# The last mLSTM head's transposed output goes from PSUM to the output projection's operands, without a round trip through DRAM

## The chip, the cores and the metric

The kernel runs on one core of one Trainium2 chip. The metric is the device time of one execution in microseconds (us). Three runs of the kernel before gave 1370.7, 1372.6 and 1374.29 us, so its median is 1372.6 us.

## What is computed

One layer of a bidirectional encoder: a combined input projection, then an attention group of 8 heads beside an mLSTM group of 4 heads, one output projection over both, and a gated feed-forward network. Cut to what matters here (1024 tokens, width 1024, mLSTM heads of 128):

```
y_attn = axial_gqa_attention(q_a, k_a, v_a, ...)                 # 512 features
h = h_fw + h_bw                                                  # per mLSTM head, 1024 x 128
h = h * rsqrt(mean(h * h) + EPS) * norm_g * sigmoid(o_pre)       # y_mem: 4 heads, 512 features
mix = concatenate([y_attn, y_mem]) @ w_out                       # the output projection
x = x + g1 * mix
h = modulate(rms_norm(x, norm_ffn_g), sh2, sc2)                  # then the feed-forward network
```

Products are made to nearly fp32 accuracy from three passes: each operand is split into a high part (rounded to fp32r) and a low part (what is left), and high x high, low x high and high x low are added up in PSUM.

## The kernel before

A Python planner writes the order of every engine's instructions: streams of matmul work (`ck.streams`) are merged by a clock with assumed costs, and chains of small steps (`ck.chain`) are put on the queues of ScalarE (ACT), VectorE (DVE), GpSimd (POOL) and SyncE (SP) as the planner's clock reaches them. The hardware then runs each engine's list strictly in that order. A step whose data are late holds up everything behind it on its engine.

**The output projection.** `MIX` (L49) lists its 32 units. A unit makes 128 output features for 512 tokens: 4 groups (k = 0 to 3) of 3 matmuls, one group for each 128 input features. The first 16 units take the attention half of the input, the last 16 the mLSTM half. In this text, unit 1.f is the mLSTM unit of feature block f (0 to 7) for tokens 512 to 1023, and unit 0.f the same for tokens 0 to 511. The planned order is: the attention units, then 1.0 to 1.7, then 0.0 to 0.7. `load_y` (L1229) provides the operands of one token half: for each k it loads a 128 x 512 tile `yat` from DRAM (`ya_d` for attention, `ym_d` for the mLSTM heads, k being the head), ACT makes the high part `yah`, POOL the low part `yal`. The weights come as `wst` from DRAM, with `whi` made by ACT and `wlo` by DVE, several units ahead. When a unit is done, DVE adds its bank into the residual (`x<-acc,mod,x`), SP stores the sum to DRAM for later (`x_d<-x`), and ACT and DVE gather the sum of squares (`sq`, `ssq`) from which the matmul `ms<-ssq` makes the mean for the second norm.

**The end of an mLSTM head.** `last` (L2010) is the chain for one head and one token half b: DVE forms `hs` from numerators and denominators, ACT squares it, DVE reduces to `ss`, POOL takes the root, and DVE multiplies by root and gate (`hs<-hs,ss,so`, four pieces). `transposed` (L2057) then turns the four 128 x 128 blocks on TensorE (PE) into one PSUM bank `tr`, ACT copies the bank, scaled by `mlstm_norm_g`, to the tile `ymt`, and SP stores that to `ym_d`. The flag `ym_ok[h][b]` releases the load in `load_y`. In `ends` (L2085) b = 1 comes before b = 0. The fourth head (h = 3) is the last one, and its turning of b = 1 lies directly ahead of the units that need it as k = 3.

**PSUM.** While the mLSTM part runs, the 8 banks are one pool with 2 banks for `acc`, 2 for `acct`, 1 for `tr` and 3 others (L2195). When the mLSTM streams are at their end (L2216) and the unit then under way is done, that pool is closed and a new one with 8 banks for `acc` is opened (L2226). The first unit planned behind that point waits for the readers of the old pool.

## Time and profile before

| what | value |
|---|---|
| three runs, median | 1372.6 us |
| the profiled execution, its own time | 1369.04 us |
| its span in the trace | 1367.2 us |
| mean granted TensorE clock | 0.983 of full |
| DVE busy | 1050.5 us (77%) |
| ACT busy | 709.6 us (52%) |
| POOL busy | 648.0 us (47%) |

The profile is one execution. Instructions carry the line of kernel.py that issued them; ACT, DVE and POOL instructions all go through one helper (L98), so they are told apart by the names of their tiles, output before input. Rows of the timeline give the start, the duration, the engine, line, operation, tiles and shapes, and in brackets how long the engine had stood idle and what released it. Consecutive matmuls overlap: in steady work at the full clock a 128x512 matmul is listed with 0.39 us, but the next one starts 0.23 us later. The time outside of the span, 1369.04 - 1367.2 = 1.84 us, is start and end.

### The profile page before, as it was taken

What the parts mean: (1) busy time and instruction counts of PE and PEld (TensorE: products, weight loads), DVE (VectorE), ACT (ScalarE), POOL (GpSimd) and SP (SyncE); (2) the same over time, 40 slices, a digit from 0 to 9 for tenths busy, and PEclk for the clock granted to TensorE, in tenths of its full rate; (3) what the DMA queues carried; (4) which work ended last, traced back from release to release, by engine and by line L of the source; (5) the groups of instructions that cost most, each with busy time, mean ns of one, the idle gap of its engine ahead of it and who ended that gap; (6) DMA issues with size and microseconds to landing.
All of it is one profiled execution on the core that took longest, in us unless ns stands there. A gap on an engine that the chain in (4) does not pass through costs nothing.

```text
span 1367.2 us, 19584 instructions
## 1 busy us (share of the span) xinstructions
PE 1278.0 (93%) x6596; PEld 1071.4 (78%) x6596; DVE 1050.5 (77%) x1599; ACT 709.6 (52%) x1344; POOL 648.0 (47%) x538
## 2 busy tenths in 40 slices
PE   7898888899999989999999999999999999979997
PEld 5786666788778879787778788888888887857887
DVE  7936698975789748989588989867666754998866
ACT  6575366778577755555377522333323334344462
POOL 0352577655667524443215255545555445545442
PEclk9999999999999999999899999999999999989999
DMA  9544333233233236763553344332333159623324
GB/s 360 160 132 129 112 106 92 88 99 107 66 94 111 65 120 199 255 202 115 179 181 116 101 143 150 123 108 100 108 108 116 71 187 349 249 78 107 100 59 158
DMA packets 105043, 188.07 MB, mean 138 GB/s; under 512 B 11632, under 2 KB 33264, under 8 KB 104944
## 3 DMA queue, kind: packets, MB, share of 16 engines
q1 hardware_dynamic: 91552, 164.73, 38.0%
q10 hardware_dynamic: 13392, 22.10, 4.3%
q8 instruction: 52, 0.85, 0.3%
q14 instruction: 47, 0.39, 0.1%
HBM read 139.86 MB, written 43.25 MB: 134 GB/s over the span
## 4 chain that ended last, share of the span: by engine, by line
PE 57%; DVE 19%; issue 8%; DMA 6%; ACT 5%; POOL 3%; SPq 1%; DVEq 0%; ACTq 0%; POOLq 0%
PE acc L314 15%; PE acc L312 15%; PE acc L313 15%; DVE sst L98 3%; DVE y L98 3%; DVE PT L98 2%; PE av L1210 2%; DVE x L98 2%; PE T L1191 2%; POOL wlo L98 1%; PE S L1159 1%; SPq L317 1%; DMA wst<-in_w_f_dram 1%; DMA wst<-in_w_gu_dram 1%; PE acct L314 1%
## 5 line engine op out<-in xcount | busy, mean ns | idle before, releaser
L98 POOL TENSOR_TENSOR wlo<-wst,whi 128x512 fp32r<-128x512 f32 (+2 forms) x165 | 238.3, 1451 | 285.1 <-ACT whi L98 271.4
L98 ACT ACTIVATE whi<-wst 128x512 fp32r<-128x512 f32 (+2 forms) x223 | 133.5, 605 | 116.6 <-PE acc L314 28.4
L313 PE MATMUL acc<-x,whi 128*128 128x512 f32 x352 | 136.9, 389 | 0.0
L98 POOL TENSOR_SCALAR P<-P,sst 128x1024 f32<-128x1024 f32 x64 | 87.0, 1360 | 86.9 <-DVE sst L98 63.0
L98 POOL TENSOR_TENSOR wlo<-wr,whi 128x512 fp32r<-128x512 f32 x52 | 72.3, 1390 | 71.0 <-ACT whi L98 67.9
L312 PE MATMUL acc<-hh,whi 128*128 128x512 f32 x224 | 96.1, 429 | 6.8 <-ACT xp L98 5.3
L312 PE MATMUL acc<-whi,wch 128*128 128x512 f32 x244 | 96.6, 396 | 5.6 <-ACT wch L98 5.6
L314 PE MATMUL acc<-whi,wcl 128*128 128x512 f32 x244 | 96.8, 397 | 2.9 <-DVE wcl L98 2.8
L313 PE MATMUL acc<-wlo,wch 128*128 128x512 f32 x244 | 96.5, 396 | 0.2
L98 ACT ACTIVATE P<-S,sst,colq 128x1024 f32<-128x1024 f32 x64 | 77.3, 1207 | 34.3 <-DVE sst L98 26.7
L98 DVE TENSOR_TENSOR PT<-T,PT 128x512 fp32r<-128x512 f32 x128 | 83.4, 681 | 9.3 <-ACT PT L98 9.1
L313 PE MATMUL acc<-hl,whi 128*128 128x512 f32 x224 | 89.5, 399 | 0.0
L314 PE MATMUL acc<-hh,wlo 128*128 128x512 f32 x224 | 89.4, 399 | 0.0
L1191 PE MATMUL T<-ident,P 128*128 128x128 f32 x512 | 71.5, 276 | 16.8 <-DVE PT L98 11.8
L98 ACT ACTIVATE whi<-wr 128x512 fp32r<-128x512 f32 x56 | 35.3, 633 | 99.0 <-DVE wr L98 48.4
L98 ACT ACTIVATE PT<-T 128x512 fp32r<-128x512 f32 x128 | 71.8, 596 | 27.4 <-PE T L1191 26.6
L98 DVE TENSOR_REDUCE sst<-S 128x1 f32<-128x1024 f32 x64 | 77.7, 1214 | 9.0 <-PE S L1159 8.9
L312 PE MATMUL acct<-whi,hh 128*128 128x256 f32 (+1 forms) x256 | 80.7, 315 | 3.7 <-ACT hh L98 2.3
L1191 PEld LDWEIGHTS T<-ident,P 128*128 128x128 f32 x512 | 58.1, 141 | 27.9 <-POOL P L98 10.3
L98 DVE TENSOR_TENSOR wcl<-wd,wch 128x512 fp32r<-128x512 f32 x50 | 50.6, 1026 | 36.9 <-ACT wch L98 36.8
L98 POOL TENSOR_TENSOR ada<-ada,cond 128x512 f32<-128x512 f32 x48 | 68.3, 1424 | 22.3 <-DMA ada<-in_w_ada_dram 22.1
L98 POOL TENSOR_TENSOR wlo<-s,whi 128x512 fp32r<-128x512 f32 x40 | 55.6, 1390 | 48.4 <-ACT whi L98 48.3
(484 smaller groups left out, 3848.8 us busy)
## 6 DMA issues: line engine op xcount, KB each, us to landing
wr<-in_w_gu_dram SPq DMA_DIRECT2D x66, 256.0 KB, 2.8
ada<-in_w_ada_dram SPq DMA_DIRECT2D x64, 256.0 KB, 3.4
wd<-in_w_d_dram SPq DMA_DIRECT2D x22, 512.0 KB, 6.5
wst<-in_w_gu_dram SPq DMA_DIRECT2D x42, 256.0 KB, 3.1
wst<-act_d SPq DMA_DIRECT2D x33, 256.0 KB, 4.1
ada<-in_w_ada_dram SPq DMA_DIRECT2D x16, 512.0 KB, 7.3
wst<-in_w_o_dram SPq DMA_DIRECT2D x32, 256.0 KB, 3.6
act_d<-sg ACTq DMA_DIRECT2D x29, 256.0 KB, 2.0
```

Source lines behind the costliest of these rows:

```text
L98: return fn(*args, **kw)
L312: nc.tensor.matmul(acc, w[0], x[0], start=first, stop=False)
L313: nc.tensor.matmul(acc, w[0], x[1], start=False, stop=False)
L314: nc.tensor.matmul(acc, w[1], x[0], start=False, stop=last)
L317: (q or nc.sync).dma_start(dst, src)
L1159: nc.tensor.matmul(sp[:, halves(n)], qs[:, j * P:(j + 1) * P], k2[g][m][:, halves(n)], start=m == 0, stop=m == 1)
L1191: nc.tensor.transpose(tp[:, k], Pt[q][:, (4 * b + k) * P:(4 * b + k + 1) * P], ident)
L1210: nc.tensor.matmul(av, va[:, k, h // 4], PT[it][m][:, k], start=(k, m) == (0, 0), stop=(k, m) == (NJ - 1, 1))
```

## The change

For the fourth head, nothing goes to DRAM. ACT reads the bank `tr`, scales by `mlstm_norm_g` and writes `yah` directly. DVE reads the same bank, scales it and subtracts `yah`, which gives `yal`. `load_y` puts these two in the place of k = 3 instead of a load. The other three heads keep their store and load. For b = 0 the high part waits until the last attention unit is done, as its load did before, since it takes a buffer of that unit's operands. With the change the bank `tr` is held until DVE has read it; before, until ACT had.

```
-    ym_d = [dram.tile([P, S], F32, name=f"ym_d{i}") for i in range(4)]
+    ym_d = [dram.tile([P, S], F32, name=f"ym_d{i}") for i in range(3)]
...
             for k in range(4):
+                if mem and k == MH - 1:
+                    Y[mem, n].append(y_last[n])
+                    continue
                 e = [None, None, Flag()]
...
         ym_ok = [[Flag(), Flag()] for _ in range(MH)]
+        y_last = [[None, None, ym_ok[MH - 1][n]] for n in range(NH)]
...
             em.set(ck, ck.t)
+            if h == MH - 1:
+                e = y_last[b]
+                src = tp.rearrange("p a b -> p (a b)")
+
+                def hi():
+                    e[0] = OPL[0].tile([P, HALF], F32R, tag="yah", name="yah", bufs=OPL[1])
+                    act.activation(e[0], src, AF.Copy, scale=V("mlstm_norm_g", h))
+
+                def lo():
+                    e[1] = OPL[0].tile([P, HALF], F32R, tag="yal", name="yal", bufs=OPL[1])
+                    dve.scalar_tensor_tensor(e[1], src, V("mlstm_norm_g", h), e[0].bitcast(F32),
+                                             op0=OP.mult, op1=OP.subtract)
+                    f.set(ck, ck.fin + LAT)
+
+                ck.chain(LAT, *yused[1:2 - b], hi, lo, flag=ym_ok[h][b])
+                return
```

On the planner's clock the new steps take other times, so the order of the instructions changes too, between the last head's first turning and unit 0.0; ahead of this stretch and behind it the order on every engine is the one of before.

On PE, before, from the group k = 2 of unit 1.0 on; the words in brackets name the engines for which a row waits:

```order
L312 MATMUL acc<-yah,whi 128x512
L313 MATMUL acc<-yal,whi 128x512 [waits Pool_49]
L314 MATMUL acc<-yah,wlo 128x512
L2062 MATMUL tr<-ident,hs 128x128 [waits DVE_49,Activation_49]
L2062 MATMUL tr<-ident,hs 128x128 [waits DVE_49] x3
L312 MATMUL acc<-yah,whi 128x512 [waits Activation_49]
L313 MATMUL acc<-yal,whi 128x512 [waits Pool_49]
L314 MATMUL acc<-yah,wlo 128x512
L312 MATMUL acc<-yah,whi 128x512 [waits DVE_49,Activation_49]
```

The second turning (b = 0) stands ahead of the group k = 3 of unit 1.0, and the last row is the first matmul of unit 1.1, the first one in the new PSUM pool.

On PE, with the change, from the same group k = 2 on:

```order
L312 MATMUL acc<-yah,whi 128x512
L313 MATMUL acc<-yal,whi 128x512 [waits Pool_49]
L314 MATMUL acc<-yah,wlo 128x512
L312 MATMUL acc<-yah,whi 128x512 [waits Activation_49]
L313 MATMUL acc<-yal,whi 128x512 [waits DVE_49]
L314 MATMUL acc<-yah,wlo 128x512
```

Here the group k = 3 follows at once, its `yah` from ACT and its `yal` from DVE. Behind it come units 1.1 and 1.2 (24 matmuls), and only then, still on PE with the change, from the last group of unit 1.2:

```order
L312 MATMUL acc<-yah,whi 128x512
L313 MATMUL acc<-yal,whi 128x512
L314 MATMUL acc<-yah,wlo 128x512
L2066 MATMUL tr<-ident,hs 128x128 [waits DVE_49,PE_49]
L2066 MATMUL tr<-ident,hs 128x128 [waits DVE_49] x3
L312 MATMUL acc<-yah,whi 128x512 [waits DVE_49]
```

The second turning has moved behind two and a quarter units. The last row is the first matmul of unit 1.3, now the first one in the new PSUM pool; the count that it waits for on DVE is that of the second `yal`, the reader of the bank which the turning just filled.

On DVE, before, from the residual addition of the last attention unit to that of unit 1.1:

```order
L98 SCALAR_TENSOR_TENSOR x_6361<-acc,mod,x_6361 128x512
L98 TENSOR_TENSOR wlo<-wst,whi 128x512
L98 TENSOR_TENSOR hs<-hs,hs_7038 128x512
L98 TENSOR_REDUCE ss<-hs_7038 128x4
L98 TENSOR_SCALAR ss<-ss 128x4
L98 TENSOR_TENSOR wlo<-wst,whi 128x512
L98 SCALAR_TENSOR_TENSOR hs<-hs,ss,so 128x128 x4
L98 SCALAR_TENSOR_TENSOR x_6224<-acc,mod,x_6224 128x512
L98 SCALAR_TENSOR_TENSOR x_6230<-acc,mod,x_6230 128x512
```

And with the change, from the row behind the last attention unit's addition to the second `yal`:

```order
L98 SCALAR_TENSOR_TENSOR yal<-tr,vec,yah 128x512
L98 TENSOR_TENSOR wlo<-wst,whi 128x512
L98 TENSOR_TENSOR hs<-hs,hs_7037 128x512
L98 SCALAR_TENSOR_TENSOR x_6223<-acc,mod,x_6223 128x512
L98 TENSOR_REDUCE ss<-hs_7037 128x4
L98 TENSOR_SCALAR ss<-ss 128x4
L98 TENSOR_TENSOR wlo<-wst,whi 128x512
L98 SCALAR_TENSOR_TENSOR x_6229<-acc,mod,x_6229 128x512
L98 SCALAR_TENSOR_TENSOR hs<-hs,ss,so 128x128 x4
L98 TENSOR_TENSOR wlo<-wst,whi 128x512
L98 SCALAR_TENSOR_TENSOR x_6270<-acc,mod,x_6270 128x512
L98 SCALAR_TENSOR_TENSOR yal<-tr,vec,yah 128x512
```

The two `yal` are new on DVE. The residual additions of units 1.0 and 1.1 (`x_6223`, `x_6229`) now stand ahead of the last product with the gate, which the second turning needs; that of 1.2 (`x_6270`) ahead of the second `yal`.

## The prediction, as put on record

> **What bounds the kernel now.** I read the page's head first, then busy time in stretches around the changed place, then the chain that ended last in that window, then the timeline of each engine there.

> ```profile
> span 1367.2 us, 19584 instructions
> ...
> PE 1278.0 (93%) x6596; PEld 1071.4 (78%) x6596; DVE 1050.5 (77%) x1599; ACT 709.6 (52%) x1344; POOL 648.0 (47%) x538
> ```

> ```profile
> 646.00:664.00 18.00, 12.65 (x39) 9.03 (x38) 7.28 (x15) 5.41 (x9) 3.43 (x3) 0.72 0.34 114
> 664.00:700.00 36.00, 36.00 (x159) 29.39 (x158) 29.57 (x44) 23.17 (x39) 5.95 (x4) 1.00 0.58 192
> 700.00:800.00 100.00, 95.98 (x414) 76.79 (x413) 91.13 (x128) 57.98 (x99) 39.74 (x25) 1.00 0.43 137
> ```

> PE is the bound: 93% of the span. Columns of a stretch are its length, busy time of PE, PEld, DVE, ACT, POOL, the granted clock, DMA share and GB/s. From 646 to 664 PE is busy for 12.65 of 18 us, at a clock of 0.72; right behind, it is busy without a break at 1.00. So there is a hole here, and time saved in it is passed on as long as PE stays the bound behind it.

> ```profile
> 643.85 0.45 PE tr L2062 x4
> 644.37 0.70 ACT ymt L98
> 645.09 2.85 DMA ym_d<-ymt
> 647.96 2.92 DMA yat<-ym_d
> 650.90 0.64 ACT yah L98
> 651.60 1.43 POOL yal L98
> 653.08 0.80 PE acc L313
> 654.34 0.76 DVE x L98
> 655.23 0.77 PE acc L312
> ```

> The chain of work through the hole is the round trip that the change takes out: store 2.85, load 2.92, high part 0.64, low part 1.43, then the first low x high product of the group k = 3 in unit 1.0. The timeline of PE gives the size of the hole:

> ```profile
> 643.69 0.60 PE L2062 MATMUL tr<-ident,hs 128*128 128x128 f32 x4
> 644.04 0.48 PE L312 MATMUL acc<-yah,whi 128*128 128x512 f32 x1
> ...
> 646.67 0.39 PE L314 MATMUL acc<-yah,wlo 128*128 128x512 f32 x1
> 651.25 1.17 PE L2062 MATMUL tr<-ident,hs 128*128 128x128 f32 x4 [4.19 <-DVE hs L98]
> 652.08 0.78 PE L312 MATMUL acc<-yah,whi 128*128 128x512 f32 x1
> ...
> 655.23 0.77 PE L312 MATMUL acc<-yah,whi 128*128 128x512 f32 x1 [0.94 <-DVE x L98]
> ...
> 660.49 0.63 PE L312 MATMUL acc<-yah,whi 128*128 128x512 f32 x1
> ...
> 663.51 0.39 PE L312 MATMUL acc<-yah,whi 128*128 128x512 f32 x1
> ...
> 677.11 0.39 PE L312 MATMUL acc<-yah,whi 128*128 128x512 f32 x1
> ```

> The rows at 655.23, 660.49, 663.51 and 677.11 are the first matmuls of units 1.1, 1.2, 1.3 and 0.0 (12 matmuls each). From 663.51 to 677.11 lie 60 of them: 0.227 us each, 2.72 us a unit. The slot behind the matmul at 646.67 is 646.90; unit 1.3 starts 16.61 us later. In between stand one turning (0.35 us, from 643.69 to 644.04) and 27 matmuls (k = 3 of 1.0, then 1.1 and 1.2), 6.12 us: 6.47 us of work. **The hole is 16.61 - 6.47 = 10.14 us.** It is made up of 4.35 until the second turning starts, 2.95 for k = 3 and its waits (3.15 + 0.83 from 651.25 to 655.23, less 0.68 and 0.35 of work), 2.54 for unit 1.1 (5.26 instead of 2.72) and 0.30 in unit 1.2. The last two are no waits but a slow clock:

> ```profile
> 651.00:655.00 4.00, 2.83 (x7) 1.45 (x7) 1.55 (x5) 1.22 (x2) 1.42 (x1) 0.50 0.18 68
> 655.00:658.00 3.00, 2.77 (x7) 2.22 (x8) 0.09 (x1) 1.15 (x2) 0.00 (x0) 0.50 0.55 175
> 658.00:661.00 3.00, 3.00 (x9) 2.32 (x8) 0.21 (x1) 0.00 (x0) 0.00 (x0) 0.50 0.00 0
> 758.00:761.00 3.00, 0.41 (x2) 0.00 (x0) 3.00 (x6) 2.73 (x7) 0.00 (x0) 1.00 0.00 0
> 761.00:764.00 3.00, 2.84 (x12) 2.18 (x12) 3.00 (x6) 2.25 (x5) 0.00 (x0) 1.00 0.23 87
> ```

> ```profile
> 761.16 0.51 PE L314 MATMUL acc<-h220h,wlo 128*128 128x512 f32 x1 [2.75 <-DVE wlo L98]
> 1201.27 0.79 PE L312 MATMUL acc<-whi,wch 128*128 128x512 f32 x1 [4.71 <-ACT wch L98]
> ```

> Behind the idle 4.19 us the clock is 0.50 for some 10 us; behind an idle 2.75 us elsewhere (761.16) it stays at 1.00, and behind 4.71 the matmul takes 0.79 us again. In this trace the limit lies between 2.75 and 4.19.

> **The change, part by part.** *The round trip of b = 1.* Gone are store, load, the copy from `yat` and POOL's subtraction. In their place: ACT writes `yah` from the bank. It starts as `ymt` did, at 644.37, takes that row's 0.70 and is done at 645.07. DVE then makes `yal`. That form, two tensors of 128x512 with one in PSUM, is the residual addition below, 0.75 us.

> ```profile
> 644.44 1.29 DVE L98 TENSOR_TENSOR hs<-num,dn 128x512 f32<-128x512 f32 x2
> 645.65 0.75 DVE L98 SCALAR_TENSOR_TENSOR x<-acc,mod,x 128x512 f32<-128x512 f32 x1
> 646.32 0.68 DVE L98 TENSOR_TENSOR wlo<-wst,whi 128x512 fp32r<-128x512 f32 x1
> 646.91 0.68 DVE L98 TENSOR_TENSOR hs<-hs,hs 128x512 f32<-128x512 f32 x1
> ...
> 650.75 1.14 DVE L98 SCALAR_TENSOR_TENSOR hs<-hs,ss,so 128x128 f32<-128x128 f32 x4 [0.91 <-POOL ss L98]
> ```

> DVE is busy until 646.32, so `yal` runs from 646.32 to 647.07; with 0.14 to reach PE (addition done at 655.09, matmul at 655.23) it is there at 647.21. PE wants it for its second matmul of the group, at 646.90 + 0.23 = 647.13. I count 0.08 us of new wait. Twelve matmuls of attention and unit 1.0 cover the rest.

> *The second turning, moved behind units 1.1 and 1.2.* PE is there at 646.90 + 27 x 0.227 + 0.08 = 653.10. Is `hs` ready? The `yal` moves the addition `hs<-hs,hs` from 646.91 to 647.57. From it to the product with the gate took 650.75 - 646.91 = 3.84 us through ACT, DVE and POOL. The additions of units 1.0 and 1.1 that DVE now does first run while DVE waits for ACT's square or for POOL's root. So the product starts at about 651.4 and ends at 652.6, before 653.10. The 4.35 us vanish, with half a microsecond in hand; and if PE does not idle, the slow clock goes too.

> *The new wait behind the turning.* Unit 1.3, the first in the new PSUM pool, waits for the second `yal`. Before, unit 1.1 was first, and waited 0.94 for the addition of 1.0. Now PE waits for a chain in series: from the start of the turning to ACT 0.68 (643.69 to 644.37), ACT 0.70, DVE 0.75, and 0.04 and 0.14 on the way: 2.31, less the turning's own 0.35: **1.96 us**. DVE is free by then: unit 1.2 ends at about 653.3, its addition at 654.1, `yal` starts at 654.5. No trace of before shows this wait. It would be 0 if nothing really held the bank. With a `wlo` (0.68) and an addition (0.75) late ahead of `yal` it would be 3.4. I take 1.96, since each link has a row.

> *What runs beside PE.* ACT does as many 128x512 steps less one per token half, POOL two subtractions less in all, DVE two steps of 0.75 more. In the units to come DVE has an addition, a `wlo` and an `ssq` for each 2.72 us of PE: 0.75 + 0.68 + 0.69 = 2.12, so it catches up. SP loses four DMAs: a weight load stood behind store and load there, and now goes earlier. The other three loads for unit 0.0 stay behind the store of unit 1.2, 12.3 us ahead of their use, and arrive within 5 to 7:

> ```profile
> 664.85 2.14 SPq L317 DMA_DIRECT2D yat<-ym_d  x4
> ...
> 670.36 5.95 POOL L98 TENSOR_TENSOR yal<-yat,yah 128x512 fp32r<-128x512 f32 x4 [17.34 <-ACT yah L98]
> ...
> 681.00 0.69 DVE L98 TENSOR_TENSOR ssq<-ssq,sq 128x512 f32<-128x512 f32 x1 [0.16 <-ACT sq L98]
> ...
> 681.87 1.02 PE L1351 MATMUL ms<-ssq,ones 128*128 128x512 f32 x2
> ```

> POOL's low parts, four in 5.95 us before, are three now; unit 0.0 comes 5 us behind the first of them as before. These costs are hidden under PE.

> *The sum.* Unit 1.3 starts at 653.10 + 0.35 + 1.96 = 655.41 instead of 663.51: **8.1 us earlier** (10.14 - 0.08 - 1.96). Behind it the order is unchanged and each load is released by a buffer that PE or its helpers free, so the rest moves as a whole. The profiled execution would take 1369.04 - 8.1 = 1360.9. The median of the runs is 3.6 us above that execution, so in its terms: 1372.6 - 8.1 = **1364.5 us**.

> **The rivals.** *The bank holds nobody up.* If the new pool's first unit does not really stand still, the gain is 10.1, 1362.5 us. Against it: before, the same place waited 0.94 us for DVE.

> *The clock falls in the new wait.* For it: the wait stands behind a turning, and adds up with it to 2.31 us, close to the 2.75 that did no harm. If it does fall, it costs again what it cost before, 2.54 + 0.30 for the matmuls and up to 0.9 around them, some 3.7 us: a gain of 4.4, 1368.2 us. [...]

> *The gain is given back.* From 700 to 800 DVE is busy for 91 of 100 us and PE waited 2.75 for a `wlo`. If loads or DVE, not PE, set that stage, it starts no earlier: 1372.6, no change. Against it: these are released by the units before them.

> *Slower, by the mean of the second norm.* Before, the last `ssq` ended at 681.69 and PE took it up at 681.87, with nothing to spare; its place in PE's order is fixed. DVE gets two steps more. If the sum of squares came later than PE, each microsecond would be lost, and the clock (3.7) once the wait passes about 3. To be slower by over 4.1 us it would have to be 8.1 + 4.1 - 3.7 = 8.5 us late. The point from which it costs anything lies some 2 us off: `ms` stands 681.87 - 677.11 = 4.76 us behind the start of unit 0.0, and the addition, the `wlo` and the `ssq` of unit 1.7, which DVE must get done in that time, are 2.12. That they needed all of it in this trace is since POOL's four subtractions ran in front of them, beside DVE's; three run now. Two steps of 0.75 do not make 8.5.

> **How the numbers follow.** My forecast has 0.73, the free bank 0.10, the fallen clock 0.08, no gain 0.06, slower 0.03. About 0.3% (4.1 us) is what a measurement of this kernel can tell from no change. The fallen clock, 1368.2, lies at that bound and is halved between faster and same: faster 0.87, same 0.10, slower 0.03. The range takes in the gain of 10.1 with 1.5 us of scatter (the three runs lie within 1.9 of their median), 1361.0, and the fallen clock, 1368.7. What it leaves out is some 0.13.

> **What would show it.** PE: no idle time worth naming between the first turning and the second; a wait of about 2 us between the second turning and unit 1.3, released by DVE's `yal`; the granted clock at 1.00 from 640 to 700; the first matmul of unit 1.3 near 655.4. DVE: two `yal` of 0.75 us. Wrong would be: idle time ahead of the second turning (`hs` late), a clock of 0.50 behind the new wait, or unit 1.3 at 655 with the end not earlier.

## The result, and the profile after

| | before | with the change |
|---|---|---|
| median | 1372.71 us (1370.08 to 1377.42, 19 runs) | 1366.48 us (1360.78 to 1370.79, 19 runs) |
| ratio of the times | | 0.9945, 95% interval 0.9933 to 0.9956 |
| profiled execution, its own time | 1369.04 us | 1367.06 us |
| its span | 1367.2 us | 1365.0 us |

The kernel became faster by 0.55%. At 1372.71 us the ratio stands for 7.5 us less, with the interval 6.0 to 9.2. The prediction said 8.1 us and 1364.5 us; the median lies 2.0 above that and inside the range.

The head of the changed kernel's page, then its busy time in the same three stretches as before and in the first two of 100 us (length, busy time of PE, PEld, DVE, ACT and POOL with counts, granted clock, DMA share, GB/s):

```profile
span 1365.0 us, 19568 instructions
...
PE 1282.9 (94%) x6596; PEld 1077.1 (79%) x6596; DVE 1052.8 (77%) x1601; ACT 708.7 (52%) x1342; POOL 644.5 (47%) x536
```

```profile
646.00:664.00 18.00, 16.44 (x76) 13.21 (x76) 16.66 (x34) 7.43 (x13) 2.28 (x4) 1.00 0.55 168
664.00:700.00 36.00, 35.34 (x154) 28.28 (x152) 29.12 (x45) 24.26 (x40) 4.64 (x3) 1.00 0.50 161
700.00:800.00 100.00, 96.67 (x412) 78.18 (x413) 89.94 (x125) 56.08 (x95) 40.46 (x26) 0.98 0.42 135
...
0.00:100.00 100.00, 85.67 (x401) 68.47 (x402) 69.73 (x132) 68.36 (x121) 29.78 (x24) 0.93 0.61 214
100.00:200.00 100.00, 88.57 (x417) 72.33 (x416) 72.60 (x85) 51.58 (x87) 49.00 (x37) 0.91 0.42 123
```

From 646 to 664 PE is now busy for 16.44 of 18 us instead of 12.65, at a clock of 1.00 instead of 0.72. Both windows hold the whole hole of their execution, and it is nearly closed. But the two spans differ by 2.2 us only, and the reason lies where the code is the same. The kernel before, its first two stretches of 100 us:

```profile
0.00:100.00 100.00, 85.55 (x413) 67.83 (x414) 69.71 (x132) 68.33 (x121) 30.77 (x25) 0.97 0.63 217
100.00:200.00 100.00, 85.13 (x414) 69.20 (x413) 73.24 (x87) 52.59 (x87) 48.10 (x36) 0.97 0.42 122
```

There the granted clock was 0.97 and 0.97, in the profiled execution of the changed kernel 0.93 and 0.91, and that one came to the first turning 4.88 us later (648.57 against 643.69). Two single executions can't be compared by their spans here. What can be compared is the time between two instructions that every version has, on either side of the change. PE's timeline of the changed kernel, start, duration, operation, and in brackets the idle time and what ended it:

```profile
648.57 0.60 PE L2066 MATMUL tr<-ident,hs 128*128 128x128 f32 x4
...
658.03 0.60 PE L2066 MATMUL tr<-ident,hs 128*128 128x128 f32 x4
660.19 0.50 PE L312 MATMUL acc<-yah,whi 128*128 128x512 f32 x1 [1.56 <-DVE yal L98]
...
678.71 1.02 PE L1354 MATMUL ms<-ssq,ones 128*128 128x512 f32 x2
```

From the first turning to unit 1.3 it takes 660.19 - 648.57 = 11.62 us; before, 663.51 - 643.69 = 19.82. **The stage became 8.20 us shorter**, where 8.1 was predicted. There is no pause left between the first turning and the second, and one new wait, from the turning's end at 658.38 (its start and 0.35 us) to 660.19: 1.81 us. For the experiments I take the way from the first turning to `ms<-ssq`, the matmul of the sum of squares: 681.87 - 643.69 = 38.18 us before, 678.71 - 648.57 = **30.14 us** now. With the 4.88 us ahead and 0.96 behind (1365.0 - 678.71 = 686.29 against 1367.2 - 681.87 = 685.33) that makes up the 2.2 us between the spans: 4.88 - 8.04 + 0.96. The last section takes up what goes with the 4.88 and the 0.96.

### The profile page after: what moved, and what is told of

Its sections match the earlier page's. It is cut to its first block, busy times and chain, and to the rows that moved or that the text cites. A ratio compares the mean times of both kernels' runs of the same rounds, so it can differ in the third digit from the quotient of the medians.

```text
span 1365.0 us, 19568 instructions
## 1 busy us (share of the span) xinstructions
PE 1282.9 (94%) x6596; PEld 1077.1 (79%) x6596; DVE 1052.8 (77%) x1601; ACT 708.7 (52%) x1342; POOL 644.5 (47%) x536
## 4 chain that ended last, share of the span: by engine, by line
PE 60%; DVE 18%; issue 7%; DMA 5%; ACT 5%; POOL 4%; SPq 1%; DVEq 0%; ACTq 0%; POOLq 0%
PE acc L312 16%; PE acc L314 16%; PE acc L313 16%; DVE sst L98 3%; DVE y L98 3%; DVE PT L98 2%; PE av L1210 2%; DVE x L98 2%; PE T L1191 2%; PE S L1159 1%; POOL wlo L98 1%; DMA wst<-act_d 1%; DMA wst<-in_w_gu_dram 1%; DVE wd L98 1%; DVE s L98 1%
## 5 line engine op out<-in xcount | busy, mean ns | idle before, releaser
L98 POOL TENSOR_TENSOR wlo<-wst,whi 128x512 fp32r<-128x512 f32 (+2 forms) x165 | 239.9, 1460 | 287.7 <-ACT whi L98 234.0
L98 ACT ACTIVATE whi<-wst 128x512 fp32r<-128x512 f32 (+2 forms) x223 | 133.6, 605 | 119.6 <-PE acc L314 28.3
L313 PE MATMUL acc<-x,whi 128*128 128x512 f32 x352 | 136.9, 389 | 0.0
L98 POOL TENSOR_SCALAR P<-P,sst 128x1024 f32<-128x1024 f32 x64 | 85.9, 1343 | 89.5 <-DVE sst L98 65.4
L98 POOL TENSOR_TENSOR wlo<-wr,whi 128x512 fp32r<-128x512 f32 x52 | 72.2, 1389 | 71.7 <-ACT whi L98 68.6
L312 PE MATMUL acc<-hh,whi 128*128 128x512 f32 x224 | 98.1, 438 | 6.9 <-ACT xp L98 5.2
L312 PE MATMUL acc<-whi,wch 128*128 128x512 f32 x244 | 96.0, 394 | 5.2 <-ACT wch L98 5.2
L314 PE MATMUL acc<-whi,wcl 128*128 128x512 f32 x244 | 96.5, 396 | 3.2 <-DVE wcl L98 3.2
L313 PE MATMUL acc<-wlo,wch 128*128 128x512 f32 x244 | 96.1, 394 | 0.5 <-POOL wlo L98 0.4
L98 ACT ACTIVATE P<-S,sst,colq 128x1024 f32<-128x1024 f32 x64 | 77.2, 1207 | 36.8 <-DVE sst L98 27.3
L313 PE MATMUL acc<-hl,whi 128*128 128x512 f32 x224 | 91.0, 406 | 0.0
L314 PE MATMUL acc<-hh,wlo 128*128 128x512 f32 x224 | 90.7, 405 | 0.0
L98 DVE TENSOR_TENSOR PT<-T,PT 128x512 fp32r<-128x512 f32 x128 | 83.3, 680 | 9.5 <-ACT PT L98 9.3
L98 ACT ACTIVATE whi<-wr 128x512 fp32r<-128x512 f32 x56 | 35.4, 632 | 100.1 <-DVE wr L98 48.3
L98 DVE TENSOR_REDUCE sst<-S 128x1 f32<-128x1024 f32 x64 | 77.7, 1213 | 12.5 <-PE S L1159 12.4
L98 ACT ACTIVATE PT<-T 128x512 fp32r<-128x512 f32 x128 | 71.7, 596 | 29.1 <-PE T L1191 28.3
L312 PE MATMUL acct<-whi,hh 128*128 128x256 f32 (+1 forms) x256 | 81.5, 318 | 4.5 <-ACT hh L98 3.1
L98 DVE TENSOR_TENSOR wcl<-wd,wch 128x512 fp32r<-128x512 f32 x50 | 50.0, 1012 | 37.9 <-ACT wch L98 29.4
L98 POOL TENSOR_TENSOR wlo<-s,whi 128x512 fp32r<-128x512 f32 x40 | 55.1, 1379 | 49.4 <-ACT whi L98 49.4
L1210 PE MATMUL av<-PT,va 128*128 128x256 f32 x512 | 71.4, 287 | 7.0 <-DVE PT L98 6.9
```

Of the source, the lines that this page charges most:

```text
L98: return fn(*args, **kw)
L312: nc.tensor.matmul(acc, w[0], x[0], start=first, stop=False)
L313: nc.tensor.matmul(acc, w[0], x[1], start=False, stop=False)
L314: nc.tensor.matmul(acc, w[1], x[0], start=False, stop=last)
L1210: nc.tensor.matmul(av, va[:, k, h // 4], PT[it][m][:, k], start=(k, m) == (0, 0), stop=(k, m) == (NJ - 1, 1))
```

## The experiments

All kernels compute the whole output. In the table, "ahead" is the start of the first turning, "way" the time from there to `ms<-ssq`, "behind" the rest of the span. The ratio is the timed one, to the kernel before on the same chip; the rows come from several batches on different chips, so ratios are compared and not medians.

| kernel | ahead | way | behind | median us | ratio, 95% interval |
|---|---|---|---|---|---|
| before | 643.69 | 38.18 | 685.33 | 1372.71 | |
| the change | 648.57 | 30.14 | 686.29 | 1366.48 | 0.9945 (0.9933 to 0.9956) |
| after_again | 647.85 | 30.12 | 685.03 | 1366.20 | 0.9952 (0.9936 to 0.9968) |
| b1_only | 644.16 | 29.44 | 684.80 | 1364.11 | 0.9934 (0.9913 to 0.9956) |
| b0_only | 646.43 | 38.97 | 687.80 | 1374.81 | 1.0013 (0.9997 to 1.0030) |
| late_pool | 646.58 | 29.52 | 686.40 | 1364.31 | 0.9933 (0.9917 to 0.9949) |
| turn_ahead | 647.01 | 38.79 | 687.00 | 1374.87 | 1.0009 (0.9985 to 1.0032) |
| warm | 644.98 | 36.69 | 684.73 | 1369.18 | 0.9980 (0.9956 to 1.0004) |
| warm2 | 648.83 | 35.08 | 686.39 | 1368.61 | 0.9970 (0.9956 to 0.9984) |
| both | 649.80 | 29.49 | 687.71 | 1365.98 | 0.9932 (0.9913 to 0.9950) |

"Ahead" scatters by 6 us and "behind" by 3, whatever the kernel; the way of the change came out as 30.14 and 30.12. So the way tells tenths of a microsecond apart that no run time of this kernel can.

### The change once more: after_again

No edit; the yardstick for the others.

> The changed kernel once more, beside the variants of this batch. Yardstick of all runs: the way on PE from the start of the last head's first turning (b = 1) to the start of the matmul ms<-ssq; it was 38.2 us before and 30.1 with the change in the two profiles at hand. Expected again: 30.1 within 0.3, a wait of 1.5 to 2.0 us between the second turning and unit 1.3, and 6 to 9 us less than before in the timed rounds. If the 8 us were an accident of one profile, the way would come out elsewhere.

The way is 30.12 us. The wait ahead of unit 1.3 is there again with the same size, and the clock stays at 1.00 behind it. PE's timeline and the stretch of that wait in this run:

```profile
659.45 0.50 PE L312 MATMUL acc<-yah,whi 128*128 128x512 f32 x1 [1.56 <-DVE yal L98]
```

```profile
658.00:661.00 3.00, 1.55 (x7) 1.29 (x8) 2.43 (x4) 3.00 (x6) 0.00 (x0) 1.00 0.73 231
```

### The change for one token half: b1_only and b0_only

Only b = 1 (or only b = 0) takes the direct way; the other keeps its store and load, and `ym_d` its four tiles.

```
-                if mem and k == MH - 1:
+                if mem and k == MH - 1 and n == 1:      (b0_only: n == 0)
...
-            if h == MH - 1:
+            if h == MH - 1 and b == 1:                  (b0_only: b == 0)
```

> Only the token half b = 1 goes from PSUM to the operands; b = 0 keeps its store and load. Theory 1 (the hole was the round trip of b = 1 ahead of the group k = 3, with the second turning in front of it): nearly the whole gain stays, way 29.5 to 30.1; the wait of unit 1.3 even shrinks from 1.8 to about 1.2, since ACT's copy alone reads the bank. Theory 2 (four DMAs less, on SP's queue and on the DMA engines, are what counts, each half alike): half the gain, way about 34.

> Only the token half b = 0 goes from PSUM to the operands; b = 1 keeps its store and load. Theory 1: no gain, way 38 to 39, since the hole in front of k = 3 of unit 1.0 stays; unit 1.1 then waits for the second yal on DVE instead of the addition alone, about 0.7 more. Theory 2: half the gain, way about 34.

Two theories stand here: one, that the gain comes from the place of the hole, b = 1's round trip and the second turning that stood in it; two, that it comes from the DMAs as such, so that either half brings its share. The ways are 29.44 and 38.97: the half b = 1 brings the whole gain and 0.7 us more, the half b = 0 nothing. The second theory falls. PE's timeline of b1_only, the second turning and unit 1.3:

```profile
653.59 0.60 PE L2066 MATMUL tr<-ident,hs 128*128 128x128 f32 x4
654.97 0.50 PE L312 MATMUL acc<-yah,whi 128*128 128x512 f32 x1 [0.78 <-ACT ymt L98]
```

PE's timeline of b0_only, the second turning and unit 1.1:

```profile
653.97 0.65 PE L2066 MATMUL tr<-ident,hs 128*128 128x128 f32 x2 [4.17 <-ACT yah L98]
...
659.02 0.77 PE L312 MATMUL acc<-yah,whi 128*128 128x512 f32 x1 [1.59 <-DVE yal L98]
```

In b1_only the second turning's bank is read by ACT alone, and unit 1.3 waits from the turning's end, 653.59 + 0.35 = 653.94, to 654.97: 1.03 us instead of 1.81. The 0.78 us in between is about the step of the bank's second reader, DVE (0.75). In b0_only the second turning still stands ahead of k = 3 and PE still idles for over 4 us there; unit 1.1 waits 1.59 us instead of 0.94.

### The second turning held at its old place: turn_ahead

The change whole, but group k = 3 of unit 1.0 is planned only when the second turning has been.

```
-                yield [y[2], pieces[w0][2]] + ([slot("acc")] if k == 0 else [])
+                yield [y[2], pieces[w0][2]] + ([slot("acc")] if k == 0 else []) + ([turned_last] if (at, f, k) == (2, 0, 3) else [])
...
+            if (h, b) == (MH - 1, 0):
+                turned_last.set(ck, ck.t)
```

> The change, but the second turning is held in its old place, ahead of the group k = 3 of unit 1.0 (units wait in the plan until it is issued). Theory 1 says that the gain needs both, no round trip and nothing in front of k = 3: PE waits for hs for some 4.7 us (hs comes 0.7 later than before, behind the first yal), the clock falls to 0.50, and the way is 37.5 to 39.5, no gain. If the round trip alone were the hole, the way would be 30 to 33.

The way is 38.79 us and the time that of before. PE's timeline, the second turning and unit 1.1, and the stretch between them:

```profile
655.62 1.17 PE L2067 MATMUL tr<-ident,hs 128*128 128x128 f32 x4 [5.26 <-DVE hs L98]
...
659.10 0.77 PE L312 MATMUL acc<-yah,whi 128*128 128x512 f32 x1 [1.03 <-DVE x L98]
```

```profile
656.00:660.00 4.00, 2.96 (x9) 1.95 (x8) 1.67 (x3) 1.57 (x3) 0.00 (x0) 0.50 0.05 18
```

Store and load are gone here too, and nothing is won: PE stands still 5.26 us for `hs`, and the clock falls to 0.50. (The pause is longer than the 4.7 us expected, since `hs` came 1.05 us later than before and not 0.7.) **Taking the round trip away brings nothing by itself; the gain comes with the move of the second turning.** That the round trip had to go for this is argued, not tested: before, PE got the low part for k = 3 at 653.08 only, 6.18 us behind the free slot at 646.90, so it would have waited there without the turning too. The reverse, the turning moved with the round trip kept, was not run.

### The old pool closed one unit later: late_pool

```
+        n_done = [0]
...
+            n_done[0] += 1
...
-        ck.streams([un], stop=lambda: not open_sum[0])
+        more = n_done[0] + 1
+        ck.streams([un], stop=lambda: not open_sum[0] and n_done[0] >= more)
```

`n_done` counts the units of the output projection. Now unit 1.4 is the first in the new pool.

> The change, with the PSUM pool closed one unit later: unit 1.3 still uses the old pool, unit 1.4 is the first in the new one. If the wait of 1.8 us behind the second turning comes from the pool's closing alone, it goes, and unit 1.4 waits about 0.95 for the addition of unit 1.3 instead: way 29.1 to 29.4, 0.9 us less than with the change. If the wait has another cause (the bank of the turning, or DVE being late), it stays at 1.8 and the way at 30.1.

The way is 29.52 us, a tenth above what was expected and 0.6 below the change. PE's timeline, second turning, unit 1.3 and unit 1.4:

```profile
656.04 0.60 PE L2068 MATMUL tr<-ident,hs 128*128 128x128 f32 x4
656.39 0.48 PE L312 MATMUL acc<-yah,whi 128*128 128x512 f32 x1
...
660.35 0.47 PE L312 MATMUL acc<-yah,whi 128*128 128x512 f32 x1 [0.94 <-DVE x L98]
```

Unit 1.3 follows the turning at once. So its wait in the change came from the new pool and from nothing that unit 1.3 itself needs. Unit 1.4 has taken it over, for 0.94 us, since the residual addition of the unit just ahead of it reads a bank of the old pool too. In PE's listed idle time the two waits are 1.56 and 0.94 us, and their difference, 0.62, is the gain in the way. The expectation was too high because it set the 0.95 of this measure against the 1.8 counted from the turning's end.

### Both: b = 1 alone and the later closing

> The change for b = 1 alone, and the old PSUM pool closed one unit later; the whole output is computed. It asks whether the two gains found so far (0.7 us by keeping the store and load for b = 0, 0.6 us by the later closing of the pool) are the same microsecond. Measure: from the start of the first turning to ms<-ssq, 30.1 us with the change, 29.44 and 29.52 with either part. If both removed the same wait ahead of the first unit in the new pool, what is left is the 0.94 us that unit 1.4 waits for the addition of unit 1.3, and the way is 29.4 to 29.6. If they were two things, the way is 28.7 to 29.0.

The way is 29.49 us, not 28.7 to 29.0: the two gains were the same microsecond. PE's timeline shows what is left, unit 1.4 behind unit 1.3's addition:

```profile
663.56 0.47 PE L312 MATMUL acc<-yah,whi 128*128 128x512 f32 x1 [0.94 <-DVE x L98]
```

late_pool, b1_only and both have ways some 0.6 to 0.7 us below the change's. Their medians lie 0.5 to 2.4 us below its 1366.48, but the intervals of the ratios overlap with the change's, so the timing alone does not show that they beat it.

### What the slow clock cost: warm and warm2

The kernel before, with throwaway bf16 matmuls that keep PE busy while it waits; their results are overwritten or never read. In warm, 18 of them ahead of the second turning, into its own bank. In warm2, into another bank, 17 ahead of the turning, 2 behind each of its first three transposes, and 4 ahead of unit 1.1.

```
+        def fill(n):
+            for _ in range(n if spin else 0):
+                nc.tensor.matmul(spin[0], identb, maskb.rearrange("p a b c -> p (a b) c"), start=True, stop=True)
...
+            if (h, b) == (MH - 1, 0):
+                spin.append(psum_any([P, 4, P], "na"))
+                fill(17)
             for j in range(4):
                 nc.tensor.transpose(tp[:, j], hs[:, j], ident)
+                fill(2 if j < 3 else 0)
...
+        fill(4)
         mlpool.__exit__(None, None, None)
```

> The kernel before, with 18 matmuls of constants (bf16, 128x512, into the bank of the turning, overwritten by it) on PE just ahead of the second turning, where PE stood idle for 4.2 us. They add work only in that idle time (18 x 0.22 = 4.0 us). If 3 to 3.7 us of the hole were the slow clock behind the idle time, the clock stays at 1.00, units 1.1 and 1.2 run at 2.72 us, and the way falls from 38.2 to 34.5 to 35.7. If the clock falls all the same, or something other than PE set the pace of unit 1.1, the way stays at 38.

The way is 36.69 us, above the 34.5 to 35.7 expected and below the 38 of the other reading. PE's timeline, the throwaway matmuls (17 of the 18 are listed), the second half of the turning, and the starts of units 1.1 and 1.2, then the stretches:

```profile
648.17 4.06 PE L2063 MATMUL tr<-maskb,identb 128*128 128x512 bf16 x17
...
653.96 0.59 PE L2065 MATMUL tr<-ident,hs 128*128 128x128 f32 x2 [0.94 <-DVE hs L98]
...
656.18 0.77 PE L312 MATMUL acc<-yah,whi 128*128 128x512 f32 x1 [0.94 <-DVE x L98]
...
660.58 0.40 PE L312 MATMUL acc<-yah,whi 128*128 128x512 f32 x1
```

```profile
652.00:654.00 2.00, 0.86 (x5) 0.32 (x3) 1.98 (x4) 0.40 (x1) 1.27 (x1) 1.00 0.00 0
654.00:656.00 2.00, 1.25 (x5) 0.65 (x5) 0.88 (x2) 0.69 (x1) 0.00 (x0) 1.00 0.00 0
656.00:658.00 2.00, 1.82 (x4) 1.50 (x5) 0.03 (x1) 0.54 (x2) 0.00 (x0) 0.53 0.74 279
658.00:660.00 2.00, 2.00 (x7) 1.61 (x6) 0.00 (x0) 0.61 (x2) 0.00 (x0) 0.61 0.40 115
```

The clock was kept through the place of the long pause, but fell at 656 all the same, for some 3.4 us; unit 1.1 took 660.58 - 656.18 = 4.40 us. Between 652.2 and 656.2 PE had made only four transposes and three matmuls, with no single pause above 0.94 us. Whether unit 1.1's slow matmuls were this clock or something else, warm2 asked.

> The kernel before with throwaway matmuls (17 ahead of the second turning, two behind each of its first three transposes, 4 ahead of unit 1.1), which write a bank that nobody reads; the whole output is computed. It asks what the slow clock by itself cost. Measure: time from the start of the first turning to the sum-of-squares matmul ms<-ssq (38.18 us before, 36.69 in the first run of this kind, where the clock fell once more behind the second turning and unit 1.1 took 4.40 instead of 2.72). If the slow clock is a term of its own, and follows the share of time in which PE works rather than a single pause, unit 1.1 takes 2.7 to 2.8 us and the way is 34.6 to 35.4, with a granted clock of 1.00 from 646 to 664. If the slow matmuls of unit 1.1 come from something else (the new PSUM pool, POOL and DVE on the same memory), unit 1.1 still takes over 4 us and the way stays 36.3 to 37.

The way is 35.08 us, as expected if it was the clock. PE's timeline, throwaway matmuls and the starts of units 1.1 and 1.2, and the same part in stretches:

```profile
658.86 1.04 PE L2061 MATMUL na<-maskb,identb 128*128 128x512 bf16 x4
660.00 0.47 PE L312 MATMUL acc<-yah,whi 128*128 128x512 f32 x1
...
662.83 0.39 PE L312 MATMUL acc<-yah,whi 128*128 128x512 f32 x1
```

```profile
656.00:658.00 2.00, 1.61 (x9) 1.08 (x10) 1.03 (x4) 0.63 (x1) 1.16 (x1) 1.00 0.06 24
658.00:660.00 2.00, 1.90 (x10) 0.88 (x8) 0.75 (x1) 0.69 (x1) 0.15 (x1) 1.00 0.03 10
660.00:662.00 2.00, 2.00 (x9) 1.66 (x10) 0.00 (x0) 0.76 (x2) 0.00 (x0) 1.00 0.79 290
```

Unit 1.1 takes 2.83 us at a clock of 1.00, with the wait for `hs` still in place: the second turning starts 7.56 us behind the first, as before. So the slow clock by itself cost 38.18 - 35.08 = 3.10 us of the hole. It could be won by busywork without the change (ratio 0.9970); the other 35.08 - 30.14 = 4.94 us only by not waiting.

## Why the prediction held, step by step

**The hole and its passing on.** 8.1 us were predicted for the stage, 8.20 measured from the first turning to unit 1.3, and 30.14 and 30.12 instead of 38.18 for the way: 0.16 of the 8.20 is lost again behind unit 1.3 (18.52 us from there to `ms<-ssq`, 18.36 before). That the rest moves as a whole holds too: what lies behind `ms<-ssq` took 685.03 and 686.29 with the change, 685.33 before.

**The k = 3 wait.** 0.08 us were predicted; the changed kernel's chain, around the first `yal`, has

```profile
651.71 0.23 PE acc L314
...
652.17 0.32 PE acc L313
...
658.19 0.45 PE tr L2066 x4
658.66 0.70 ACT yah L98
659.38 0.76 DVE yal L98
660.19 0.50 PE acc L312
```

0.32 instead of 0.23 for the low x high product, so 0.09 us.

**`hs` in time for the moved turning.** This was the weakest step and it held by less than I counted. Predicted: product with the gate 7.7 us behind the first turning (651.4 - 643.69). DVE's timeline of the changed kernel:

```profile
651.19 0.74 DVE L98 SCALAR_TENSOR_TENSOR yal<-tr,vec,yah 128x512 fp32r<-128x512 f32 x1
...
652.44 1.10 DVE L98 TENSOR_TENSOR hs<-hs,hs 128x512 f32<-128x512 f32 x1
...
656.70 1.14 DVE L98 SCALAR_TENSOR_TENSOR hs<-hs,ss,so 128x128 f32<-128x128 f32 x4 [0.24 <-POOL ss L98]
...
675.65 0.69 DVE L98 TENSOR_TENSOR ssq<-ssq,sq 128x512 f32<-128x512 f32 x1 [0.16 <-ACT sq L98]
```

The product started 8.13 us behind it (656.70 - 648.57). The addition took 1.10 us instead of 0.68, with POOL at work on the gate from 0.18 us ahead of it. Before and in warm, warm2 and b0_only POOL's step on the gate began 0.06 to 0.56 us behind the addition's start, and the addition took 0.68 or 0.69 us. POOL's row in the changed kernel:

```profile
652.26 0.75 POOL L98 TENSOR_SCALAR so<-so 128x512 f32<-128x512 f32 x1 [6.12 <-ACT so L98]
```

The product ended at 657.84, and PE came to the turning at 658.03: 0.19 us in hand where I had counted 0.5. The room was a little larger than that, as the turning can begin on the first of the four pieces: before, it began at 651.25, inside the product (650.75 to 651.89).

**The new wait.** 1.96 us predicted, 1.81 measured, and the chain above is the predicted one link by link: turning, ACT 0.70, DVE 0.76, matmul. b1_only (1.03 without DVE's link) and late_pool (none at unit 1.3) show that it is the readers of the old pool's banks. `yal` took 0.74 us (the row at 651.19) where 0.75 was taken from the residual addition.

**The rivals.** The bank does hold PE up, so 10.1 us was out of reach. The clock did not fall in the new wait, in the profiles of the change, of after_again and of b1_only. The gain was not given back. And `ms<-ssq` was not late: the last `ssq` that it needs (the row at 675.65) ended at 676.34, 2.4 us ahead of the matmul at 678.71, where before it was 0.18.

**What stood too narrow.** The prediction put the clock's limit as an idle time between 2.75 and 4.19 us. The warm run contradicts this: there the clock fell with no pause above 0.94 us. The 2.75 us that "did no harm" were luck of one trace: with the change the same wait for the same `wlo` is again 2.75 us long, and behind it the clock is 0.50. So it was right that the clock would outlast the new wait, but a limit on the idle time is not what the runs show; the last section has what they do show. And the slow clock counted as 2.84 to 3.7 us measured 3.10.

**The median.** Medians of 19 runs differ by 6.2 us, the ratio gives 7.5 and the way 8.0. The scatter of single runs (10 us from the fastest to the slowest with the change) is larger than these differences, and 8.0 lies inside the interval of the ratio.

## What to carry to other kernels

A round trip that stands on the critical chain may be worth only what waits beside it: ask which other instruction is free to move once it is gone, since in turn_ahead the round trip alone brought nothing. Here a PSUM pool was closed and opened again in the middle of matmul work, and the first unit in the new one waited for readers of the old: PE's listed idle time there was 1.56 us with the change, 0.78 in b1_only, 0.94 (at unit 1.4) in late_pool. So close it away from a turning and its slow reader chain. A pause of 2.75 us was followed by a clock of 1.00 in one execution and of 0.50 in another (see below), so one trace does not tell what a pause costs. And measure such a change between two instructions that both versions share, since the whole run scatters by more than the change is worth.

## What the runs showed of the hardware that was not expected

  The steps lie differently in the two traces, so a pause falls into one window or is cut in two. The wait of 2.75 us for `wlo` is the example; PE's row with the change (the one of before, at 761.16, stands in the prediction):

```profile
757.97 0.50 PE L314 MATMUL acc<-h220h,wlo 128*128 128x512 f32 x1 [2.75 <-DVE wlo L98]
```

  The two windows around that wait, before:

```profile
756.70:760.11 3.41, 1.71 (x7) 0.86 (x5) 3.41 (x7) 2.85 (x6) 0.00 (x0) 1.00 0.00 0
760.11:763.53 3.42, 2.37 (x10) 1.99 (x11) 3.42 (x7) 2.80 (x6) 0.00 (x0) 1.00 0.11 41
```

  And with the change, the window of the wait and the next one:

```profile
755.53:758.94 3.41, 0.97 (x4) 0.85 (x5) 3.41 (x6) 3.09 (x6) 0.00 (x0) 1.00 0.00 0
758.94:762.36 3.42, 3.42 (x9) 2.69 (x9) 3.42 (x7) 1.15 (x2) 0.00 (x0) 0.50 0.20 77
```

  Before, the wait is shared out (0.50 and 0.69 busy) and the clock stays; with the change one window takes most of it (0.28) and the next is at half clock. "Behind" is 685.33 us before and 686.29 with the change; how much of these 0.96 us the fall makes was not measured. The new wait ahead of unit 1.3, listed as 1.56 us, leaves by estimate at least 3.41 - 1.56 = 1.85 us of a window, 0.54, however the steps lie. That is above the 0.48 from which on the clock stayed at 1.00 behind all windows but one, though not by much.
- DVE's product with the gate took 2.15 us instead of 1.14 when POOL made a `yal` at the same time. The warm run, DVE's timeline and then POOL's:

```profile
652.02 2.15 DVE L98 SCALAR_TENSOR_TENSOR hs<-hs,ss,so 128x128 f32<-128x128 f32 x4 [0.91 <-POOL ss L98]
```

```profile
652.48 1.27 POOL L98 TENSOR_TENSOR yal<-yat,yah 128x512 fp32r<-128x512 f32 x1 [0.50 <-ACT yah L98]
```

  The extra microsecond is close to the 1.27 of POOL's step. In b0_only the product took 2.15 too, with POOL's 1.28 inside it. It took 1.14 before and in warm2, where POOL's `yal` began 0.85 and 0.95 us behind its start, and with the change, with POOL idle. No run took POOL's step away alone, so this is a reading of the rows, not a test.
- With the same code ahead of it, the first turning came between 643.69 and 649.80 us. The granted clock differs with it: up to 640 us the trace of before has 20.5 us at 0.50, that of the change 47.8. From 100 to 200 us the mean was 0.97 before; b1_only, warm, b0_only, late_pool and turn_ahead had 0.93 to 0.97 and came to the turning at 644.16 to 647.01; the four latest, from 647.85 to 649.80, had 0.91. It does not explain the order within these groups: turn_ahead, with 0.97, is the last of its five. What else moves the start was not looked into.
